# Order of the matrix products in a weights-stationary block: second part of the weights directly behind the first

## The chip, the core and the metric

The kernel runs on one core of a Trainium2 chip. The metric is the device time of one execution in microseconds, and the median of several runs is compared. A core has a matrix engine (TensorE, PE in the profile, with a row PEld for its weight loads), VectorE (DVE), ScalarE (ACT), GpSimd (POOL) and SyncE (SP), which here issues the loads from memory. Each engine works through its own instructions in order and waits on semaphores for the others.

## The reference

One layer of a diffusion backbone on 256 latent tokens and 256 context tokens of 2048 channels, all in float32. Cut to what matters here:

```python
mod = silu(c) @ w_mod + b_mod                      # shift, scale, gate
h  = modulate(rms_norm(x), shift, scale)
p_i, p_ff, p_fb, p_q, p_g, p_cv, p_cg, p_gc, p_gh = split_proj(h @ w_in)
o  = hgrn_bidir(q_prep(p_q), p_i, forget(p_ff), forget(p_fb), s_f, s_b)   # gated recurrence, 8 heads
y_h = (rms_norm(o) * silu(p_g)) @ w_o
y_c = silu(layer_norm(axial_dwconv(p_cv * sigmoid(p_cg)))) @ w_pw
x  = x + gate * rms_norm((sigmoid(p_gc) * y_c + sigmoid(p_gh) * y_h) @ w_out)
h2 = modulate(rms_norm(x), shift2, scale2)
x  = x + gate2 * rms_norm(square(relu(h2 @ w1)) @ w2)
```

The context tokens go through part of the same projection and give the recurrence's starting states s_f and s_b.

## The kernel before

**Numbers in two parts.** Every weight and every activation is split into a first part (hi, rounded to the matrix engine's fast float32 form) and the rest (lo). A product of two such numbers is taken as hi·hi + hi·lo + lo·hi, so three products stand for one.

**The weights' stream.** `Stream` brings the weights in pieces of 128 x 1024 float32 (512 KB), in the order in which they are used. `prepare` takes one piece: ScalarE copies it to `whi` (line 123), VectorE subtracts to get `wlo` (line 126). There are four buffers for each of the two (`AHEAD`, lines 117 and 118), and five for the raw pieces (line 81), which SyncE loads (line 85). `next` (line 129) keeps four pieces prepared, so the buffer of the piece in use now is filled again for the piece four later.

**Two ways to multiply.** In `tokens` (line 277) the activations are the stationary operand and the weights stream through, 512 columns at a time, by `mm3r`. In `blocks` (line 263) the weights are stationary: a piece holds eight blocks of 128 input rows and 128 output channels (cut(0) to cut(7)), and `mm2` (line 246) multiplies them with the activations of 256 tokens. For each of the eight the activation operand x(k) is 512 wide: hi of the 256 tokens, then lo. `mm2` first runs eight products with the eight blocks of whi over all 512 columns (line 252), which give hi·hi in the bank's first half and hi·lo in its second. Then it runs eight products with the blocks of wlo over the hi half alone, 256 columns, added to the bank's second half (line 254). `total` (line 225) adds the two halves when the bank is done: ScalarE copies the second half (line 228), VectorE adds (line 229).

**Where mm2 runs.** With 2048 inputs an output block takes two pieces, so two calls of `mm2`, and `blocks` calls it 160 times: 16 for the queries (line 735), 32 for the convolution's gate and value (lines 767 and 787), and for the MLP's first matrix 16 in the first quarter and 32 in each of the other three (line 995). Between the calls, `pump` lets other work in: steps of the recurrence's heads (`head`, with its small products at line 1391, each behind a copy `left` on ScalarE at line 1380 and products of x on VectorE at lines 1398, 1406 and 1407), the convolution, and sums for the gates (lines 1231 and 1244).

**What sets the order.** Each engine gets its instructions in the order of the program text as the generators emit it, with a few `issue_after` marks. A buffer is filled again only when its last reader is done: whi when the last product of line 252 in its call is done, wlo when the last of line 254 is.

Of the kernel before, what the change touches and what calls it, by code (L numbers as in the profile page):

```python
# [136 lines left out]
class Kernel:  # L137
# [108 lines left out]
    def mm2(self, bank, w, x, ks, nk):  # L246


        nc = self.nc
        cut = lambda i: slice(i * P, (i + 1) * P)  # L250
        for i, k in enumerate(ks):
            nc.tensor.matmul(bank, w[0][:, cut(i)], x(k)[2], start=(k == 0), stop=False)  # L252
        for i, k in enumerate(ks):
            nc.tensor.matmul(bank[:, T:], w[1][:, cut(i)], x(k)[0], start=False, stop=(k == nk - 1))  # L254

    def mm3r(self, out, x, w, first, last):
# [79 lines left out]
    def cut(self, pages, tb, c):  # L336

        return pages[2 * tb + c // 2][:, (c % 2) * 512:(c % 2 + 1) * 512]
# [1280 lines left out]
```

## Time and profile before

| | |
|---|---|
| median of 3 runs | 1643.31 us (1642.83 to 1644.01) |
| the profiled execution | 1643.43 us |
| its span, first to last instruction | 1641.7 us |
| granted TensorE clock | 1.000 |
| products of line 252 (512 columns) | 1280 |
| products of line 254 (256 columns) | 1280 |
| memory traffic | 227 GB/s over the span |

The profile is of one execution. Its times are microseconds from the span's start; durations of single instructions are in nanoseconds where a mean is given. A line `L252 PE MATMUL bank<-h,whi 128*128 128x512 f32 x1280 | 322.3, 394 | 0.0` says: line 252, TensorE, a product that writes bank from h and whi, 128 x 128 stationary, 128 x 512 moving, 1280 of them; together 322.3 us busy, 394 ns each; the engine idle 0.0 us just before them. Products overlap, since the next one begins before the one before has drained, so what a product costs is the distance from its start to the next one's. In a timeline several like instructions in a row are one line with their count. The chain that ended last is followed back from the last instruction, at each step to what released it.

### The profile page before, as it was taken

The numbers are of one execution on the slowest core, as the hardware profiler recorded it, in microseconds if no ns is written. First come the engines' busy times: TensorE is split into PE (matmuls) and PEld (weight loads), VectorE is DVE, ScalarE is ACT, GpSimd is POOL, SyncE is SP. The second block draws the span as 40 slices with busy tenths as digits, with TensorE's granted clock in tenths as the row PEclk, the third lists the DMA queues.
The fourth block names the chain that finished last, engine by engine and source line by source line (L and its number), as shares of the span: only waits on it lengthen the run. The fifth ranks groups of instructions, "written<-read, shape, count | busy, mean of one in ns | idle before, by whom it ended". The sixth has DMA issues, their size and how long they took to land.

```text
span 1641.7 us, 22004 instructions
## 1 busy us (share of the span) xinstructions
PE 1627.7 (99%) x8207; PEld 1357.7 (83%) x8207; DVE 1163.2 (71%) x1702; ACT 799.7 (49%) x1141; POOL 8.1 (0%) x18
## 2 busy tenths in 40 slices
PE   8999999999999999999999999999999999999998
PEld 6668888888988888888788888888888888888887
DVE  7777877777868889967887766456655665566555
ACT  6553444343554444653446665445544554346543
POOL 0000000000000000000000000000000000000000
PEclk9999999999999999999999999999999999999999
DMA  9998954444656566678887466677666666665553
GB/s 378 392 395 293 316 166 141 154 142 142 207 189 224 187 192 206 230 271 306 313 289 260 143 230 205 214 235 241 218 206 231 234 213 217 230 219 195 190 193 116
DMA packets 103484, 374.47 MB, mean 228 GB/s; under 512 B 11601, under 2 KB 11857, under 8 KB 103377
## 3 DMA queue, kind: packets, MB, share of 16 engines
q1 hardware_dynamic: 101952, 368.60, 65.8%
q0 software_dynamic: 1280, 4.21, 0.8%
q8 instruction: 64, 1.05, 0.3%
q14 instruction: 44, 0.35, 0.1%
q10 hardware_dynamic: 144, 0.26, 0.0%
HBM read 370.93 MB, written 2.10 MB: 227 GB/s over the span
## 4 chain that ended last, share of the span: by engine, by line
PE 94%; DVE 2%; DMA 2%; ACT 1%; issue 1%; SPq 0%; DVEq 0%; ACTq 0%
PE bank L185 62%; PE bank L252 18%; PE bank L254 9%; PE bank L1391 2%; DMA x<-ctx 1%; DVE wlo L126 1%; DMA rawpage<-wm 1%; PE bank L1422 0%; DMA raw<-wpw 0%; PE bank L1433 0%; PE bank L1431 0%; ACT whi L123 0%; ACT h L629 0%; SPq L498 0%; ACT xT L629 0%
## 5 line engine op out<-in xcount | busy, mean ns | idle before, releaser
L126 DVE TENSOR_TENSOR wlo<-raw,whi 128x1024 fp32r<-128x1024 f32 x488 | 594.0, 1223 | 356.2 <-ACT whi L123 348.0
L123 ACT ACTIVATE whi<-raw 128x1024 fp32r<-128x1024 f32 x488 | 513.5, 1059 | 576.9 <-PE bank L185 320.7
L185 PE MATMUL bank<-whi,h 128*128 128x512 f32 x1264 | 396.3, 391 | 0.8 <-ACT h L629 0.5
L252 PE MATMUL bank<-h,whi 128*128 128x512 f32 x1280 | 322.3, 394 | 0.0
L185 PEld LDWEIGHTS bank<-whi,h 128*128 128x128 f32 x1264 | 237.1, 188 | 51.0 <-DVE h L1080 0.7
L252 PEld LDWEIGHTS bank<-h,whi 128*128 128x128 f32 x1280 | 230.4, 189 | 41.6
L185 PE MATMUL bank<-wlo,h 128*128 128x512 f32 x632 | 246.5, 390 | 0.8 <-DVE wlo L126 0.8
L185 PE MATMUL bank<-whi,hidh 128*128 128x512 f32 x503 | 195.1, 388 | 0.0
L185 PE MATMUL bank<-wlo,hidh 128*128 128x512 f32 x503 | 195.1, 388 | 0.0
L185 PE MATMUL bank<-whi,hidl 128*128 128x512 f32 x503 | 195.0, 388 | 0.0
L254 PEld LDWEIGHTS bank<-h,wlo 128*128 128x128 f32 x1280 | 174.6, 190 | 12.6
L254 PE MATMUL bank<-h,wlo 128*128 128x256 f32 x1280 | 178.4, 282 | 0.0
L185 PE MATMUL bank<-h,whi 128*128 128x512 f32 x512 | 164.6, 402 | 0.0
L185 PEld LDWEIGHTS bank<-wlo,h 128*128 128x128 f32 x632 | 118.7, 188 | 26.6 <-DVE wlo L126 2.5
L185 PEld LDWEIGHTS bank<-whi,hidl 128*128 128x128 f32 x503 | 94.4, 188 | 19.5
L185 PEld LDWEIGHTS bank<-wlo,hidh 128*128 128x128 f32 x503 | 94.5, 188 | 19.3
L185 PEld LDWEIGHTS bank<-whi,hidh 128*128 128x128 f32 x503 | 94.5, 188 | 19.2
L185 PEld LDWEIGHTS bank<-h,whi 128*128 128x128 f32 x512 | 92.0, 189 | 21.5 <-issue 5.9
L185 PE MATMUL bank<-h,wlo 128*128 128x512 f32 x256 | 100.0, 391 | 0.0
L1244 DVE SCALAR_TENSOR_TENSOR raw<-raw,silu_row 128x1024 f32<-128x1024 f32 x64 | 76.6, 1218 | 0.2 <-DMA raw<-wmt 0.2
L1231 DVE SCALAR_TENSOR_TENSOR gacc<-raw,silu_c,gacc 128x1024 f32<-128x1024 f32 x60 | 76.6, 1277 | 0.0
L185 PEld LDWEIGHTS bank<-h,wlo 128*128 128x128 f32 x256 | 48.1, 188 | 10.6 <-DVE wlo L126 0.3
(246 smaller groups left out, 1359.8 us busy)
## 6 DMA issues: line engine op xcount, KB each, us to landing
raw<-w SPq DMA_DIRECT2D x256, 512.0 KB, 4.2
raw<-wi SPq DMA_DIRECT2D x172, 512.0 KB, 4.4
raw<-wmt SPq DMA_DIRECT2D x64, 512.0 KB, 4.2
raw<-wm SPq DMA_DIRECT2D x64, 512.0 KB, 4.5
rawpage<-wm SPq DMA_DIRECT2D x48, 512.0 KB, 8.6
raw<-wo SPq DMA_DIRECT2D x32, 512.0 KB, 4.8
raw<-wmd SPq DMA_DIRECT2D x16, 512.0 KB, 8.2
raw<-who SPq DMA_DIRECT2D x16, 512.0 KB, 4.9
```

What stands on the lines that cost most here:

```text
L123: kn.his.append(nc.scalar.activation(out=hi, in_=raw, func=AF.Copy))
L126: kn.los.append(nc.vector.tensor_tensor(lo, raw, hi.bitcast(F32), op=ALU.subtract))
L185: ins = fn(*args, **kw)
L252: nc.tensor.matmul(bank, w[0][:, cut(i)], x(k)[2], start=(k == 0), stop=False)
L254: nc.tensor.matmul(bank[:, T:], w[1][:, cut(i)], x(k)[0], start=False, stop=(k == nk - 1))
L1231: nc.vector.scalar_tensor_tensor(acc, raw, s, acc, op0=ALU.mult, op1=ALU.add)
L1244: nc.vector.scalar_tensor_tensor(raw, raw, 1.0, self.srow, op0=ALU.mult, op1=ALU.mult, accum_out=self.dot[:, 32 * j + b:32 * j + b + 1])
L1391: nc.tensor.matmul(ps[:, b * P:(b + 1) * P], w, r, start=True, stop=True)
```

## The change

In `mm2` the second loop's header is taken out, so that each product with wlo follows at once on the product with whi of the same block:

```diff
         cut = lambda i: slice(i * P, (i + 1) * P)
         for i, k in enumerate(ks):
             nc.tensor.matmul(bank, w[0][:, cut(i)], x(k)[2], start=(k == 0), stop=False)
-        for i, k in enumerate(ks):
             nc.tensor.matmul(bank[:, T:], w[1][:, cut(i)], x(k)[0], start=False, stop=(k == nk - 1))
```

The product with wlo is then at line 253. Number, size and operands of the products are the same; only their order within a call of `mm2` differs: long, short, long, short, in place of eight long and eight short.

## The prediction

> **What bounds the kernel now.** I read the page first, then its chain that ended last, then the timeline of single stretches.
>
> ```profile
> span 1641.7 us, 22004 instructions
> PE 1627.7 (99%) x8207; PEld 1357.7 (83%) x8207; DVE 1163.2 (71%) x1702; ACT 799.7 (49%) x1141; POOL 8.1 (0%) x18
> PE 94%; DVE 2%; DMA 2%; ACT 1%; issue 1%; SPq 0%; DVEq 0%; ACTq 0%
> PE bank L185 62%; PE bank L252 18%; PE bank L254 9%; PE bank L1391 2%; DMA x<-ctx 1%; DVE wlo L126 1%; DMA rawpage<-wm 1%; PE bank L1422 0%; DMA raw<-wpw 0%; PE bank L1433 0%; PE bank L1431 0%; ACT whi L123 0%; ACT h L629 0%; SPq L498 0%; ACT xT L629 0%
> L252 PE MATMUL bank<-h,whi 128*128 128x512 f32 x1280 | 322.3, 394 | 0.0
> L254 PE MATMUL bank<-h,wlo 128*128 128x256 f32 x1280 | 178.4, 282 | 0.0
> ```
>
> TensorE is the chain: 94% of it, and lines 252 and 254, the two that the change reorders, are 27% of it, some 443 us. Both rows end in 0.0: TensorE never stood idle before one of these products. So a change here counts only by how closely the 2560 products follow one another, or by a wait that it makes. The mean durations (394 and 282 ns) overlap each other, so I take differences of start times.
>
> ```profile
> 1101.70 1.98 PE L252 MATMUL bank<-h,whi 128*128 128x512 f32 x8
> 1103.51 1.11 PE L254 MATMUL bank<-h,wlo 128*128 128x256 f32 x8
> 1104.46 2.00 PE L252 MATMUL bank<-h,whi 128*128 128x512 f32 x8
> 1106.08 1.13 PEld L254 LDWEIGHTS bank<-h,wlo 128*128 128x128 f32 x8
> 1106.31 1.12 PE L254 MATMUL bank<-h,wlo 128*128 128x256 f32 x8
> 1107.14 1.70 PEld L252 LDWEIGHTS bank<-h,whi 128*128 128x128 f32 x8
> 1107.26 2.00 PE L252 MATMUL bank<-h,whi 128*128 128x512 f32 x8
> ...
> 1188.26 2.00 PE L252 MATMUL bank<-h,whi 128*128 128x512 f32 x8
> ```
>
> The columns are start, extent, engine and line. From the eight long products at 1104.46 to those at 1188.26 lie 30 calls of mm2: 83.80 / 30 = 2.793 us each, or **349.2 ns for a pair** of one long (512 columns) and one short (256). Inside a call, the long run takes 1106.31 - 1104.46 = 1.85 us and the short run 0.95 us. The first call of the stretch has 1103.51 - 1101.70 = 1.81 us for the same eight long ones.
>
> What one product costs when nothing but its own kind is around it comes from two other stretches, 21 long products in a row and 32 short ones (the tail's 256-column halves):
>
> ```profile
> 1274.30 0.39 PE L185 MATMUL bank<-whi,hidh 128*128 128x512 f32 x1
> ...
> 1279.06 1.98 PE L252 MATMUL bank<-h,whi 128*128 128x512 f32 x8
> ...
> 1629.11 0.40 PE L185 MATMUL bank<-wpage,hidh 128*128 128x256 f32 x2
> ...
> 1632.95 0.28 PE L185 MATMUL bank<-whi,hidl 128*128 128x256 f32 x1
> ```
>
> Long: 4.76 / 21 = 226.7 ns. Short: 3.84 / 32 = 120.0 ns. Their difference is 106.7 ns for 256 columns, so each product costs its columns at 0.417 ns plus 13.3 ns, whatever its length. A pair of settled products is 346.7 ns, 2.773 us for eight; mm2 takes 2.793. So **20 ns of each call belong to the switches**, and the rows say which: eight long ones after short ones take about 1.84 us instead of 1.81 (27 ns too many), and eight short ones 0.95 instead of 0.96 (about 7 too few). The long products pay after short ones everywhere; here they follow the last call of a stretch:
>
> ```profile
> 1191.06 0.40 PE L185 MATMUL bank<-whi,hidh 128*128 128x512 f32 x1
> 1191.29 0.40 PE L185 MATMUL bank<-wlo,hidh 128*128 128x512 f32 x1
> 1191.53 0.39 PE L185 MATMUL bank<-whi,hidl 128*128 128x512 f32 x1
> 1191.76 0.40 PE L185 MATMUL bank<-whi,hidh 128*128 128x512 f32 x1
> 1191.99 0.39 PE L185 MATMUL bank<-wlo,hidh 128*128 128x512 f32 x1
> 1192.22 0.39 PE L185 MATMUL bank<-whi,hidl 128*128 128x512 f32 x1
> ```
>
> Five products take 1.16 us where settled ones take 1.133, with other operands and at another line: the same 27 ns, spread over about five products, and then it is over. The first two carry most of it (0.47 us for two, 235 ns each).
>
> **The change, part by part.** It adds and removes no instruction: 160 calls issue the same 1280 + 1280 products with the same loads. It moves the short products, and with them two events: the first use of wlo comes earlier and the last use of whi later.
>
> *The cadence.* After the change every long product follows one short one, and every short one follows one long one. The trace has no such alternation, so its price needs bounds from both sides.
> - Lower end: the long one settled (226.7) and the short one as the first of a run. The short run is 7 ns too quick as a whole, and all of that would be its first product's: 113 ns. Pair 340, which is 9.2 less than now: 1280 x 9.2 = 11.8 us saved.
> - Upper end: every long one as the slowest after a run (235) and every short one at the run's 120: pair 355, 5.8 more: 7.4 us lost.
> - Value taken: each product as the first after a switch: the long one about 233 (226.7 + 6.5), the short one 113; their sum is 346.5 and thus again the sum of the settled ones, 346.7. That is the nearest row, since after the change each product is the first after a switch, and two ways of reading give it. It saves 20 ns a call. Five of the 160 calls come after long products and have 1.81 already, so 155 x 20 ns = **3.1 us saved**.
>
> *wlo earlier.* The short product's weights are now needed 0.23 us after the call begins and not 1.85 us. VectorE makes them behind ScalarE's whi:
>
> ```profile
> 1101.63 4.74 DVE L126 TENSOR_TENSOR wlo<-raw,whi 128x1024 fp32r<-128x1024 f32 x4 [5.57 <-ACT whi L123]
> 1106.51 1.06 ACT L123 ACTIVATE whi<-raw 128x1024 fp32r<-128x1024 f32 x1 [1.58 <-PE bank L252]
> 1107.60 1.23 DVE L126 TENSOR_TENSOR wlo<-raw,whi 128x1024 fp32r<-128x1024 f32 x1 [1.23 <-ACT whi L123]
> ACT whi L123 <- PE bank L252: 129.8, 86, 2.4
> ```
>
> The wlo that is ready at 1107.60 + 1.23 = 1108.83 belongs to the call four further on than that of 1104.46, at 1104.46 + 4 x 2.793 = 1115.63: a lead of 7.0 us even for the second product. The tightest place is the start of a stretch: the four made from 1101.63 serve the calls from 1104.46 on, and the first is done at about 1102.82. It leads the second product by 1.9 us. Price nothing; the cover would have to shrink by 1.9 us before it cost anything.
>
> *whi held longer.* ScalarE waits for the last long product before it overwrites a whi (86 times, the row above). That product now starts 7 x 0.347 = 2.43 us into the call instead of 1.85 - 0.23 = 1.62, so whi, the wlo behind it, and all that VectorE and ScalarE have queued behind these are 0.8 us later. The raw buffer comes free 0.8 us later too, and SP's loads that wait for it. The weights' lead of 7.0 us becomes 6.2. What has no such lead is the recurrence's heads between the calls near 460 us:
>
> ```profile
> 455.71 1.06 ACT L123 ACTIVATE whi<-raw 128x1024 fp32r<-128x1024 f32 x1
> 459.92 0.39 ACT L1380 COPY left<-x 128x256 f32<-128x256 f32 x1
> 456.80 1.23 DVE L126 TENSOR_TENSOR wlo<-raw,whi 128x1024 fp32r<-128x1024 f32 x1 [2.98 <-ACT whi L123]
> 458.27 0.55 DVE L1406 TENSOR_TENSOR x<-x,fg 128x384 f32<-128x384 f32 x1
> 458.74 0.55 DVE L1407 TENSOR_TENSOR x<-x,fg 128x384 f32<-128x384 f32 x1
> 460.36 0.71 PE L1391 MATMUL bank<-x,left 128*128 128x128 f32 x4 [0.49 <-ACT left L1380]
> PEld bank L1391 <- ACT left L1380: 2.9, 8, 0.7
> ```
>
> whi, wlo, the two products of x, left, and then TensorE, which already waits 0.49 us: a whi that is 0.8 us later makes it wait 0.8 us more. The last row counts eight such waits of the weight load in the whole kernel, most of which cost TensorE nothing. Bounds: 0 and 8 x 0.8 = 6.4 us; I take one, **0.8 us lost**, since one such wait stopped TensorE itself.
>
> Sum, against the profiled execution's own 1643.43 us (span 1641.7, 1.7 around it): 1643.4 - 3.1 + 0.8 = **1641.1 us**. The median shown is 1643.31, the same within its scatter. A measurement of this kernel can tell about 0.2% (3.3 us) from no change, so the forecast lies within that, near its lower edge: with the 0.8 in it, faster begins at a pair of 346.0 and slower at 351.2.
>
> **The rivals.**
> - *The alternation runs clean* (340 to 346 a pair). In a run of short products the next load begins as soon as a product has begun, with no pause between loads; in the alternation a load has a long product's time every second turn. For it: the load of 1107.14 starts with the last short product (1107.26 - 0.12), so the short ones are paced by loads that press on each other, and the first one, before which the load had time, is quicker. Against it: long products need about five of their kind to settle, and now never get two. Time at its end 1643.4 - 11.8 + 0.8 = 1632.4; at 343 a pair 1636.3. The Trainium skill ("TensorE: Matmul & The Clock Gate", "Architectural detail: the array is 16× 32×32, not 1× 128×128") says that TensorE's queue can pull weight loads ahead of running matmuls, which favours this rival; the trace agrees that loads are pulled ahead, but shows them ahead by one product only.
> - *The order is indifferent*: a long product owes 27 ns for eight short ones before it, 3.4 for each, and pays as much one by one. The pair stays 349.2 and the time is 1643.4 + 0.8 = 1644.2. For it: the five-product tail looks like a debt being paid. Against it: the 7 ns of the first short product come back eight times. The same page ("LDWEIGHTS (loading the stationary operand)") gives a load of 128 columns 107 ns, an estimate by which no load outlasts either product and no order matters; measured short products at 120.0 show that something more is paid.
> - *Slower: neither settles.* Every long product pays what the first two after a run pay (233 to 235) and the short one costs the 120 of the middle of a run, as if two loads always pressed on each other. Place: all 1280 pairs; price at 354 a pair 1280 x 4.8 = 6.1 us, time 1643.4 + 6.1 + 0.8 = 1650.3. It decides from a pair of 351.2 on. For it: seven of the eight short ones in a run do cost 120, and the slow start of the long ones is regular. Against it: a short one right after a long one has been the quick one.
> - *The heads' waits multiply* to the eight above: 1643.4 - 3.1 + 6.4 = 1646.7, just slower. Against it: only one of the eight stopped TensorE.
>
> **How the numbers follow.** Forecast and the indifferent order together, pairs of 346.0 to 351.2: 0.41 (0.28 and 0.13), all within 0.2%. Clean alternation below 346.0: 0.37, faster. Neither settles: 0.17, and the heads' waits: 0.05, slower. So faster 0.37, same 0.41, slower 0.22; the likeliest is the forecast, 1641.1. For the range I leave out the last tenth at each end: below, the cleanest runs under 341 a pair (1643.4 - 10.5 + 0.8 = 1633.7, rounded 1633.5); above, the unsettled ones over 352.5 (1643.4 + 4.2 + 0.8 = 1648.4, rounded 1648.5). The likeliest sign's own range, 346.0 to 349.2, is 1640.1 to 1644.2.
>
> **What would show it.** In the changed kernel's timeline, lines 252 and 253 alternate one by one; eight pairs should take 2.77 us from call to call (2.72 clean, 2.79 indifferent, 2.83 unsettled). Their rows should still end in idle 0.0. ScalarE's whi at such a call should start 0.8 us later against its beginning, and the wait for left near 460 us should grow from 0.49 to about 1.3 us. The prediction is wrong if the pair isn't near 346.7, if TensorE waits for wlo at line 253, or if the heads wait more than twice.

## The result and the profile after

| | before | after |
|---|---|---|
| median of 9 runs | 1644.01 us (1642.83 to 1645.35) | 1647.89 us (1647.25 to 1649.56) |
| ratio after / before | | 1.0025, interval 1.0016 to 1.0034 |
| the profiled execution, its span | 1643.43 us, 1641.7 us | 1647.25 us, 1645.5 us |
| granted TensorE clock | 1.000 | 1.000 |

The changed kernel is a quarter of a per cent slower: the sign that the rival *neither settles* gave, not the forecast's. The page of after, in the parts that were read of before (busy time, the chain's shares, the two groups of products):

```profile
span 1645.5 us, 22006 instructions
PE 1630.8 (99%) x8207; PEld 1356.9 (82%) x8207; DVE 1163.3 (71%) x1702; ACT 798.9 (49%) x1141; POOL 8.1 (0%) x18
PE 92%; DMA 3%; DVE 3%; ACT 1%; issue 1%; SPq 0%; DVEq 0%; ACTq 0%
L252 PE MATMUL bank<-h,whi 128*128 128x512 f32 x1280 | 454.0, 400 | 0.0
L253 PE MATMUL bank<-h,wlo 128*128 128x256 f32 x1280 | 359.6, 281 | 0.0
```

TensorE is busy 3.1 us longer (1630.8 for 1627.7) and the span is 3.8 us longer; the other engines are where they were. Both groups still end in idle 0.0, so no wait has come in front of these products. That their busy sums grew by 130 and 180 us says nothing of the cost: that is the overlap of neighbours, which alternate now. The cost is in the distance of starts, in the timeline of TensorE (start, extent, engine, line), here inside a call and then at the beginnings of two calls:

```profile
1118.90 0.40 PE L252 MATMUL bank<-h,whi 128*128 128x512 f32 x1
1119.14 0.28 PE L253 MATMUL bank<-h,wlo 128*128 128x256 f32 x1
1119.26 0.40 PE L252 MATMUL bank<-h,whi 128*128 128x512 f32 x1
1119.49 0.28 PE L253 MATMUL bank<-h,wlo 128*128 128x256 f32 x1
1119.61 0.40 PE L252 MATMUL bank<-h,whi 128*128 128x512 f32 x1
1119.84 0.28 PE L253 MATMUL bank<-h,wlo 128*128 128x256 f32 x1
1119.96 0.40 PE L252 MATMUL bank<-h,whi 128*128 128x512 f32 x1
```

```profile
1105.12 0.40 PE L252 MATMUL bank<-h,whi 128*128 128x512 f32 x1
...
1187.10 0.40 PE L252 MATMUL bank<-h,whi 128*128 128x512 f32 x1
```

Three pairs take 1119.96 - 1118.90 = 1.06 us, and 29 calls take 81.98 us: 2.827 us a call, **353.3 ns a pair** where before had 349.2 and the forecast 346.7. In nanoseconds the trace's start times repeat every three pairs:

```
long 232, short 118 | long 240, short 120 | long 236, short 114     sum 1060
```

But the same trace holds other calls, between steps of the recurrence's heads:

```profile
490.75 0.39 PE L252 MATMUL bank<-h,whi 128*128 128x512 f32 x1
...
512.94 0.39 PE L252 MATMUL bank<-h,whi 128*128 128x512 f32 x1
```

Eight calls in 22.19 us: 2.774 us each, **346.7 ns a pair**, with long products at 230 and short ones at 117. So the alternation has two patterns, and one of them is what was forecast. I call them quick and slow. Of the 160 calls, 125 run at 2.81 to 2.83 us, 13 at 2.78 or less, and 22 begin behind products of other work, after which the first long product takes 313 to 379 ns. The 13 quick ones all lie in the stretches of the convolution's gate and value.

The sums of all calls, from a call's first start to the start of what follows its last product, show where the time went:

| stretch | before, us | after, us |
|---|---|---|
| queries, 16 calls | 44.67 | 45.21 |
| gate, 16 | 46.52 | 45.82 |
| value, 16 | 45.13 | 44.90 |
| MLP, first quarter, 16 | 45.01 | 45.54 |
| MLP, each other quarter, 32 | 89.36 | 90.43 |

Together that is 3.4 us of the 3.8 between the two profiled executions. About as much as the rest is there before any reordered product runs: the first of them, in the queries, starts at 167.15 us before and at 167.66 after. The gate's stretch gains 0.7 us: there the wait of TensorE near 460 us is gone.

### The profile page after: what moved, and what is told of

It is laid out like the page before. It is cut to its first block, busy times and chain, and to the rows that moved or that the text cites. A ratio compares the mean times of both kernels' runs of the same rounds, so it can differ in the third digit from the quotient of the medians.

```text
span 1645.5 us, 22006 instructions
## 1 busy us (share of the span) xinstructions
PE 1630.8 (99%) x8207; PEld 1356.9 (82%) x8207; DVE 1163.3 (71%) x1702; ACT 798.9 (49%) x1141; POOL 8.1 (0%) x18
## 3 DMA queue, kind: packets, MB, share of 16 engines
q0 software_dynamic: 1280, 4.21, 0.7%
q8 instruction: 64, 1.05, 0.3%
## 4 chain that ended last, share of the span: by engine, by line
PE 92%; DMA 3%; DVE 3%; ACT 1%; issue 1%; SPq 0%; DVEq 0%; ACTq 0%
PE bank L185 60%; PE bank L252 18%; PE bank L253 9%; PE bank L1390 2%; DMA rawpage<-wm 1%; DVE wlo L126 1%; DMA raw<-wf 1%; DMA x<-ctx 1%; PE bank L1421 0%; DMA raw<-wpw 0%; PE bank L1432 0%; PE bank L1430 0%; DMA raw<-wmd 0%; ACT h L628 0%; SPq L497 0%
## 5 line engine op out<-in xcount | busy, mean ns | idle before, releaser
L252 PE MATMUL bank<-h,whi 128*128 128x512 f32 x1280 | 454.0, 400 | 0.0
L253 PE MATMUL bank<-h,wlo 128*128 128x256 f32 x1280 | 359.6, 281 | 0.0
L252 PEld LDWEIGHTS bank<-h,whi 128*128 128x128 f32 x1280 | 241.0, 188 | 57.6
L253 PEld LDWEIGHTS bank<-h,wlo 128*128 128x128 f32 x1280 | 242.1, 189 | 0.2
L185 PE MATMUL bank<-h,whi 128*128 128x512 f32 x512 | 164.8, 403 | 0.0
L185 PEld LDWEIGHTS bank<-h,whi 128*128 128x128 f32 x512 | 92.1, 189 | 21.5 <-issue 5.9
L185 PEld LDWEIGHTS bank<-h,wlo 128*128 128x128 f32 x256 | 48.1, 188 | 10.6 <-DVE wlo L126 0.3
```

The costliest lines, as they stand in the source:

```text
L185: ins = fn(*args, **kw)
```

## The experiments

Four explanations of the two patterns stood against each other; where an expectation uses a letter, it is one of these.
- **A**: weight loads and products fall into one of two lasting rhythms, and what goes ahead of the alternation decides which.
- **B**: a product pays for adding to the columns of the bank that the one before it has just written.
- **C**: the operands' places in memory decide, so that a given call is always quick or always slow.
- **D**: each return from short to long products costs a fixed amount.

In most of these kernels `mm2` takes its order from a table, call by call (digits are the eight blocks of whi, letters those of wlo):

```diff
-        for i, k in enumerate(ks):
-            nc.tensor.matmul(bank, w[0][:, cut(i)], x(k)[2], start=(k == 0), stop=False)
-            nc.tensor.matmul(bank[:, T:], w[1][:, cut(i)], x(k)[0], start=False, stop=(k == nk - 1))
+        ks = list(ks)
+        group = self.groups.popleft() if len(self.groups) > 1 else self.groups[0]
+        order = {1: "0a1b2c3d4e5f6g7h", 2: "01ab23cd45ef67gh", 4: "0123abcd4567efgh", 8: "01234567abcdefgh", "skew": "01a2b3c4d5e6f7gh"}[group]
+        for o in order:
+            i = "01234567abcdefgh".index(o)
+            k = ks[i % 8]
+            if i < 8:
+                nc.tensor.matmul(bank, w[0][:, cut(i)], x(k)[2], start=(k == 0), stop=False)
+            else:
+                nc.tensor.matmul(bank[:, T:], w[1][:, cut(i - 8)], x(k)[0], start=False, stop=(k == nk - 1))
```

Order 1 is that of after, 8 that of before. `groups` is set ahead of each stretch; its last entry holds for all calls that follow. With this text the long product is at line 258 and the short one at 260. "q1" to "q3" are the MLP's second to fourth quarter, "q0" its first.

### Several orders in one kernel (e1_groups)

```diff
+        self.groups = collections.deque([8])
...
+        self.groups = collections.deque([1])
...
+            self.groups = collections.deque([[1], [2], [4], ['skew']][q])
```

The first line stands ahead of the queries, the second ahead of the gate and of the value, the third ahead of the MLP's quarter q.

> Order differs by stretch: queries eight-eight, MLP quarter 0 one-one, quarter 1 two long and two short in turn, quarter 2 four and four, quarter 3 one-one shifted by one (long 0, long 1, short 0, long 2, short 1, ..., short 7). Theory A (a pair's price is a repeating pattern of TensorE that the stretch falls into at its entry): 2.793 us a call in the queries, 2.827 in quarter 0, as before and after; two-two and four-four pay the first steps after each switch (long 233, 236, 228, 232; short 113, 119, 120, 120), 2.804 both; shifted either near 2.773 or near 2.83. Rival B (the short product is slowed, or slows the next long one, because it adds to the columns that were written just before): 6.7 ns for each long product that follows a short one beside 2.773, so two-two 2.80, four-four 2.787, shifted 2.82. Rival D (a fixed price of 20 ns for each switch back to long): two-two 2.853, four-four 2.813.

1644.69 us, 1644.83 for before beside it. The queries took 2.793 us a call (order 8), q0 2.827 where nothing interrupts (order 1), q3 2.818 and 2.822 in turn (skewed). Calls of two and two in q1, then of four and four in q2, in the timeline of TensorE:

```profile
1104.64 0.40 PE L258 MATMUL bank<-h,whi 128*128 128x512 f32 x1
...
1188.24 0.62 PE L258 MATMUL bank<-h,whi 128*128 128x512 f32 x2
...
1281.79 0.63 PE L258 MATMUL bank<-h,whi 128*128 128x512 f32 x2
...
1365.99 0.63 PE L258 MATMUL bank<-h,whi 128*128 128x512 f32 x2
```

30 calls each: 83.60 / 30 = 2.787 us and 84.20 / 30 = 2.807. No set of numbers in the expectation is hit as a whole. The order is not monotonic (2.793, 2.807, 2.787 and 2.827 for groups of eight, four, two and one), so **D is out**: a fixed price for each return would rise with their number.

### Other columns of the bank (e2_half)

```diff
-            nc.tensor.matmul(bank[:, T:], w[1][:, cut(i)], x(k)[0], start=False, stop=(k == nk - 1))
+            nc.tensor.matmul(bank[:, :T], w[1][:, cut(i)], x(k)[0], start=False, stop=(k == nk - 1))
```

> The changed kernel, but the product with wlo adds to the first half of the bank in place of the second, which gives the same sum of both halves. Each half was last written at another distance in time. Theory A: nothing moves, 2.827 us a call in the MLP's quarters, total about 1647. Rival B (same columns written just before): the pair moves off 353.3, towards 346.7 (2.773 a call) if the second half's freshness is what costs.

1648.23 us. In q1, first products of two calls:

```profile
1106.09 0.40 PE L252 MATMUL bank<-h,whi 128*128 128x512 f32 x1
...
1190.89 0.40 PE L252 MATMUL bank<-h,whi 128*128 128x512 f32 x1
```

84.80 / 30 = 2.827 us, unchanged: it doesn't matter which half the short product adds to. That takes one form of B away, not all of it, since the long product before has just written both halves. The rest of B falls with e4_first below, where the same products on the same columns cost 346.7 or 353.3 ns a pair.

### Small products ahead of a stretch (e3_lead)

```diff
                     hi, lo = self.stream.next()
+                    for _ in range(self.lead if b0 == first and j == h == 0 else 0):
+                        self.nc.tensor.matmul(accs[0][:, :P], self.v["ident"], self.v["ident"], start=True, stop=True)
```

`lead` is 8 for the queries and 1, 2, 3, 4 for the MLP's quarters, 0 elsewhere.

> The changed kernel, with a few small products (128x128 float32, into a bank that is cleared right after) ahead of the first product of a stretch only: queries 8, MLP quarters 0 to 3 with 1, 2, 3 and 4. Theory A: the entry decides, so at least one of the five stretches holds 2.773 us a call (346.6 a pair) to its end, while others stay at 2.827. Rivals B and C (C: the operands' places in memory decide): all five stay at 2.827 from the second call on. The small products themselves cost about 0.1 us each.

1652.89 us. All five stretches ran at 2.827 us a call behind their first one: a miss. The trace holds 36 of the extra products at line 271, about 112 ns apart, two for each of the eighteen in the text; that is 4 of the 5 us above after. So the numbers that ran were 16, 2, 4, 6 and 8: none of these makes the alternation quick, and no odd number was tried.

### One call of another order, then the change's order (e4_first)

```diff
+        self.groups = collections.deque([8, 1])
...
+            self.groups = collections.deque([[4, 1], [2, 1], [8, 1], ['skew', 1]][q])
```

> The changed kernel, but the first call of a stretch has another order: eight-eight in the queries and in MLP quarter 2, four-four in quarter 0, two-two in quarter 1, shifted by one in quarter 3; all later calls one-one. Theory A: some of these entries give 2.773 us a call for all the later calls, others 2.827. Rivals B and C: 2.827 in every stretch from the second call on.

1645.21 us. The timeline of TensorE from the beginning of the second call on, in q1 (behind two and two) and then in q2 (behind eight and eight); the rows left out alternate in the same way:

```profile
1104.77 0.40 PE L258 MATMUL bank<-h,whi 128*128 128x512 f32 x1
1105.01 0.28 PE L260 MATMUL bank<-h,wlo 128*128 128x256 f32 x1
...
1105.82 0.39 PE L258 MATMUL bank<-h,whi 128*128 128x512 f32 x1
...
1281.49 0.40 PE L258 MATMUL bank<-h,whi 128*128 128x512 f32 x1
1281.73 0.28 PE L260 MATMUL bank<-h,wlo 128*128 128x256 f32 x1
...
1282.56 0.40 PE L258 MATMUL bank<-h,whi 128*128 128x512 f32 x1
```

Three pairs of the same order take 1.05 us behind the one call and 1.07 behind the other, and it lasts: q1 ran at 2.773 us a call in all its 31 later calls, q2 at 2.827. Behind four and four (q0) the calls were quick until other products came between them, behind the skewed order (q3) slow. q1 is the stretch that ran slow in after, with the same operands: **C is out**, and so is what was left of B. Of **A** it is shown that what goes ahead decides and that in these undisturbed stretches the pattern then stays; that loads and products make the rhythm between them is not shown by this run (two runs with half loads, below, bear on it).

### The quick entry everywhere (e5_two_first), a mixed call (e6_mixed), two and two (e7_twos)

Three whole kernels, eleven runs each. The first has one call of two and two at the head of the queries and of each quarter of the MLP (its lines are shown); the second takes the order "01ab2c3d4e5f6g7h" in every call; the third has two and two in all calls.

```diff
+        self.groups = collections.deque([2, 1])
...
+            self.groups = collections.deque([[2, 1], [2, 1], [2, 1], [2, 1]][q])
```

> The changed kernel, but in the queries and all four MLP quarters the first call of the stretch goes two long, two short in turn; all later calls one-one. Theory A: every one of these stretches then holds 2.773 us a call until other products come between two calls (quarter 0, and once in quarter 3); some 110 to 120 calls save 0.054 us against the changed kernel, so 6 us: about 1641.5 to 1642.5 where before is 1644, ratio 0.998 to 0.999. If quarter 1 of the last experiment was chance, some stretches run at 2.827 and the time is above that of before.

> Every call goes two long, two short, and then six pairs one-one, so that each call brings its own entry, also after other products. Theory A: the two-two part costs its switches (the all-two-two quarter had 2.787) and the rest 346.7 a pair: 2.773 to 2.785 a call in every stretch, gate and value stretches included, about 1641.5. Against it: a two-two part in the middle of the quick pattern may throw it out again, 2.80 to 2.83.

> Every call two long and two short in turn. From the quarter measured with this order: 2.787 a call everywhere, 6 ns less than before and 40 less than after: about 1 us below before, 1643, ratio 0.999 to 1.000.

| kernel | median of 11, us | before beside it, us | ratio, interval |
|---|---|---|---|
| e5_two_first | 1642.32 | 1644.37 | 0.9986 (0.9977 to 0.9995) |
| e6_mixed | 1644.57 | 1644.37 | 1.0001 (0.9992 to 1.001) |
| e7_twos | 1643.05 | 1644.37 | 0.9992 (0.9983 to 1.0001) |

Beginnings of the second and the thirty-second call of q1 in e5_two_first, in its timeline:

```profile
1103.76 0.40 PE L258 MATMUL bank<-h,whi 128*128 128x512 f32 x1
...
1186.96 0.40 PE L258 MATMUL bank<-h,whi 128*128 128x512 f32 x1
```

83.20 / 30 = **2.773 us a call**, the forecast's number. The queries, q1 and q2 ran so throughout; q0 only until other work came between the calls at 978 us, and q3 up to its fourteenth call (about 1492 us). In all, 111 calls were quick, 27 slow, and 22 began behind other products. With five changed calls the order of after is 2.1 us below before; after was 3.9 above it, so in all the five calls are worth about 6 us, from two comparisons. By call sums, half of the gain over before is not the entries': 0.9 of 1.8 us lies in the gate's and the value's stretches, which run as in after.

In the mixed kernel the calls took turns:

```profile
1106.02 0.63 PE L258 MATMUL bank<-h,whi 128*128 128x512 f32 x2
1106.49 0.39 PE L260 MATMUL bank<-h,wlo 128*128 128x256 f32 x2
...
1108.80 0.62 PE L258 MATMUL bank<-h,whi 128*128 128x512 f32 x2
1109.26 0.40 PE L260 MATMUL bank<-h,wlo 128*128 128x256 f32 x2
...
1111.62 0.63 PE L258 MATMUL bank<-h,whi 128*128 128x512 f32 x2
```

2.78 us, then 2.82, and so on, where 2.773 to 2.785 was expected: two and two is no key by itself. Where its two short products took 116 and 113 ns the pairs behind them were quick; where they took 113 and 119 they were slow. A call that is entered from slow pairs comes out the first way and one entered from quick pairs the second, so they take turns. The two and two of e7_twos stays at 2.787 us a call, as expected; its interval includes no change against before.

### Entering again behind the interruption (e9_reenter)

e5_two_first, with two and two again in the ninth call of q0 and the fifteenth of q3, behind the interruptions.

```diff
+            self.groups = collections.deque([[2, 1, 1, 1, 1, 1, 1, 1, 2, 1], [2, 1], [2, 1], [2, 1, 1, 1, 1, 1, 1, 1, 1, 1, 1, 1, 1, 1, 2, 1]][q])
```

> As the kernel with two long, two short in the first call of the queries' and MLP's stretches, and the same order again for the call after an interruption: the ninth call of quarter 0 and the fifteenth of quarter 3. Theory A: 2.773 us in the 17 calls of quarter 3 behind it, where it was 2.827, and possibly in the last seven of quarter 0: 0.9 to 1.3 us less, about 1641.2, ratio 0.998. If the place in the stretch mattered and not the entry, quarter 3 stays at 2.827 there.

1642.24 us, before 1644.09, ratio 0.9988 (0.9979 to 0.9997): no gain over e5_two_first. Both calls ended on short products of 113 and 119 ns, and the calls behind them ran slow, as the mixed kernel's reading says; this run's expectation missed. The groups inside these calls show why: the two short products of the four groups take 116 and 112, 113 or 114 and 119, 116 and 112 or 113, 113 and 119 ns. Each group of two and two turns one state into the other, and four of them, entered from slow pairs, come back to slow. Entered from settled long products, four end on 116 and 112 (e5_two_first). One group behind slow pairs leads to quick ones in every second call of the mixed kernel; no run used that behind an interruption and then kept to one-one.

### Half a weight load for the short products (e8_cols), for the long ones (e10_long_cols)

In e8_cols 15 of 16 short products load 64 columns of weights in place of 128 (queries, q1, q2); the output channels left out lack that part of the lo·hi term. In e10_long_cols 14 of 16 long products do, in the same stretches, which leaves out half of what they add. Queries run in order 8, q1 in order 1, q2 in order 1 behind a first call of two and two; q0 and q3 keep whole loads, q3 in order 1 behind a first call of four and four. Where a load is halved, the product that uses it is half as wide too, so these runs can't tell the one from the other.

```diff
+                n = self.cols if k < nk - 1 else P
+                nc.tensor.matmul(bank[:n, T:], w[1][:, cut(i - 8)][:, :n], x(k)[0], start=False, stop=(k == nk - 1))
...
+                n = self.cols if 0 < k < nk - 1 else P
+                nc.tensor.matmul(bank[:n], w[0][:, cut(i)][:, :n], x(k)[2], start=(k == 0), stop=False)
```

> Measures what the weight load adds. In the queries (order eight-eight), MLP quarter 1 (one-one) and quarter 2 (two-two first, then one-one) 15 of 16 short products use only 64 of their 128 weight columns, which leaves half of that correction out; quarter 0 one-one and quarter 3 four-four first, then one-one, whole. If the 13.3 ns that each product takes beside its columns is the weight load running next to it, half a load takes 6.7: in the queries the settled short product falls from 120.0 to 113.3 and the long ones stay at 226.7; in the quick pattern a pair falls from 346.7 to about 340. If the 13.3 ns belong to the product itself, nothing moves. Theory A says nothing on the size in the slow pattern, but a load that is shorter changes the phase, so quarter 1 may leave 353.3. Quarter 3 should hold 2.773 by its four-four entry.

> The counterpart: 14 of 16 long products use only 64 of their 128 weight columns (half of what these would add is left out), the short ones all 128. Queries eight-eight, MLP quarter 1 one-one, quarter 2 two-two first and then one-one; quarters 0 and 3 whole (one-one, and four-four first). If a short product is paced by the load that runs next to it, it costs 113.3 beside a half load: with the long one's 226.7 the pair is 340, 2.72 us a call, in quarters 1 and 2, apart from the full-width ones. If not the load but the short product itself is slow, the pair stays near 347. In the queries the long ones stay at 226.7, the short run at 120.

One run each: 1640.92 and 1640.9 us. Queries of e8_cols, the eights of a whole call:

```profile
203.30 2.00 PE L258 MATMUL bank<-h,whi 128*128 128x512 f32 x8
205.14 1.08 PE L261 MATMUL bank<-h,wlo 128*64 128x256 f32 x8
206.06 2.00 PE L258 MATMUL bank<-h,whi 128*128 128x512 f32 x8
```

The short run takes 0.92 us (before: 0.95), settled products 113 to 114 ns for 120; the long run still takes 1.84, its slow beginning unchanged. In q1 every call took 2.772 to 2.778 us, behind long products too, and so did those of q2 from its third on (the second 2.790): the slow pattern is gone. But 2.777 us is 347 ns a pair; the 340 that were expected for the quick pattern did not come.

q2 of e10_long_cols, pairs with half and then with whole weights for the long product, and two of the weight loads (PEld):

```profile
1183.18 0.39 PE L259 MATMUL bank<-h,whi 128*64 128x512 f32 x1
1183.40 0.28 PE L261 MATMUL bank<-h,wlo 128*128 128x256 f32 x1
...
1184.20 0.39 PE L259 MATMUL bank<-h,whi 128*64 128x512 f32 x1
...
1184.76 0.28 PE L261 MATMUL bank<-h,wlo 128*128 128x256 f32 x1
1184.77 0.19 PEld L259 LDWEIGHTS bank<-h,whi 128*128 128x128 f32 x1
1184.88 0.40 PE L259 MATMUL bank<-h,whi 128*128 128x512 f32 x1
1185.11 0.28 PE L261 MATMUL bank<-h,wlo 128*128 128x256 f32 x1
1185.23 0.40 PE L259 MATMUL bank<-h,whi 128*128 128x512 f32 x1
1185.47 0.28 PE L261 MATMUL bank<-h,wlo 128*128 128x256 f32 x1
1185.47 0.14 PEld L259 LDWEIGHTS bank<-h,whi 128*64 128x64 f32 x1
1185.59 0.40 PE L259 MATMUL bank<-h,whi 128*64 128x512 f32 x1
1185.82 0.28 PE L261 MATMUL bank<-h,wlo 128*128 128x256 f32 x1
1185.94 0.39 PE L259 MATMUL bank<-h,whi 128*64 128x512 f32 x1
```

Three pairs with half the load take 1184.20 - 1183.18 = 1.02 us: 340 ns a pair, 227 + 113. Two whole loads for long products in a row (those of 1184.88 and 1185.23) make the next three pairs (233 + 117) + (241 + 119) + (233 + 117), 1.06 us. So the half loads take away both the short product's 117 to 120 ns and the long one's 233 to 241.

What a whole load costs does not fall on the product beside it. Each load starts beside the product before its own. The short product at 1184.76 has the first whole load beside it (1184.77) and takes 1184.88 - 1184.76 = 0.12 us, 113 ns in the trace's nanoseconds; the one at 1185.47 has a half load beside it and takes 119. In the same way the first short product of before's runs has a whole load beside it and takes 113. The cost comes a product or two late and is spread over long and short ones.

In the queries, where half loads run beside the long products of a run, eight of them take 1.84 us (the starts' differences are 224 to 236 ns), in the first call too, where whole loads took 1.81. The expectation of settled 226.7 missed there, and no run shows why.

q3 of both kernels, with whole loads, ran quick in all its 31 later calls, as expected, also behind the interruption at its fourteenth call. First products of the fifteenth and the last call of e8_cols:

```profile
1493.36 0.40 PE L258 MATMUL bank<-h,whi 128*128 128x512 f32 x1
...
1540.51 0.40 PE L258 MATMUL bank<-h,whi 128*128 128x512 f32 x1
```

47.15 / 17 = 2.774 us a call, where e5_two_first and e9_reenter ran at 2.827. Behind four and four the long products take 230 ns and the short ones 117, behind two and two 231, 112, 233 and 117 in turn: two forms of the quick pattern with the same sum, and here the first form was followed by quick calls behind the interruption and the second by slow ones.

## Why the prediction was wrong, and where it was right

**The cadence: the value taken failed.** The bounds, 340 to 355, hold both patterns that came, and the quick one has the value taken, 346.7, though not its parts: the long products take 230 ns and the short ones 117, not 233 and 113. What failed is the step "each product as the first after a switch", with about 233 and 113 as its fixed price. That takes a product's cost to depend on its kind and its neighbour. The runs show that it depends on the state in which the alternation is entered: the same products in the same order cost 346.7 or 353.3 a pair, for a whole stretch (e4_first). From long products, with which the clean stretches start, or from a call of eight and eight it goes to 353.3. Before's undisturbed calls can't show this, since their switches are eight products apart and the long ones settle in between.

**The split of the two costs failed too.** The forecast read 226.7 and 120.0 as 0.417 ns a column and 13.3 ns whatever the length. In rows of half loads a short product takes 113 (e8_cols' queries, e10_long_cols' pairs), half of a settled long one's 226.7: 0.443 ns a column and no fixed part that these rows show. Long products don't get cheaper with half loads beside them (226 to 230 in most of e8_cols' pairs). So the settled short product's other 6.7 ns go with whole loads that follow one another closely. They are not a price that each short product pays for the load beside it, since the first of a run has a whole load beside it and takes 113; from before's rows one couldn't tell how much of them an alternation would bring back.

**The rival that came true** is *neither settles*, given 0.17. It asked for 354 a pair and put the point of decision at 351.2; measured 353.3 in the slow pattern, and from call sums 125 x 33 ns = 4.2 us more in the slow calls (2.827 less 2.793 us each). Its reason was only half right: the short products (118, 120, 114) come near what the middle of a run costs, but the long ones go up to 240, which no long product of a run in before's undisturbed calls does.

**The clean alternation** (340 to 346) did not come with these loads; its lower end, 340, is what e10_long_cols shows with half the long products' loads. The Trainium skill ("TensorE: Matmul & The Clock Gate", "Architectural detail: the array is 16× 32×32, not 1× 128×128") says that weight loads can be pulled ahead of running matmuls. The runs agree: each load starts beside the product before its own (the load for the product of 1184.88 at 1184.77 in e10_long_cols). They also show that this is not free: 120.0 ns a product in a run of short ones with whole loads, 113 to 114 with half ones.

**The order is indifferent** (349.2) fell: e1_groups alone has four different costs for four orders. The 107 ns of its estimate are not what the trace shows of a load: those of lines 252 and 254 last 189 and 190 ns on average, so a load does outlast the 113 to 120 ns from a short product to the next.

**wlo earlier: right.** Line 253 ends in idle 0.0, as the price of nothing had it.

**whi held longer: right in its size, wrong in the chain behind it.** ScalarE near 460 us, first before and then after (the bracket is the idle time before and what ended it), with TensorE's products of after:

```profile
458.95 1.06 ACT L123 ACTIVATE whi<-raw 128x1024 fp32r<-128x1024 f32 x1 [2.19 <-PE bank L252]
459.92 0.39 ACT L1380 COPY left<-x 128x256 f32<-128x256 f32 x1
```

```profile
457.60 1.06 ACT L123 ACTIVATE whi<-raw 128x1024 fp32r<-128x1024 f32 x1 [0.75 <-PE bank L252]
459.55 0.41 ACT L1379 COPY left<-x 128x256 f32<-128x256 f32 x1 [0.89 <-DVE x L1406]
460.82 1.06 ACT L123 ACTIVATE whi<-raw 128x1024 fp32r<-128x1024 f32 x1 [0.86 <-PE bank L252]
460.74 0.61 PE L1390 MATMUL bank<-x,left 128*128 128x128 f32 x4
```

whi starts 2.95 us behind its call's beginning (457.60 after 454.65), where before had 458.95 - 456.82 = 2.13: 0.8 later, as predicted. But the chain whi, wlo, x, left of the forecast is not what held left in before. There the second x had ended at 458.74 + 0.55 = 459.29, and left started only at 459.92, directly behind a whi on ScalarE itself that had waited 2.19 us for the long products of line 252. In after, left stands ahead of the next whi: it starts at 459.55, as soon as x is done, and the products of line 1390 start at 460.74 behind no wait, in place of 0.49 us of it. So instead of 0.8 us lost, the gate's stretch gained 0.7. Each engine works through its instructions in order, so this is another order of them: the traces of before and after differ in it here on ScalarE and on VectorE, although their program text is the same. That the text alone sets the order is therefore too simple, and what moved it is not shown.

**The sum.** Forecast -3.1 and +0.8; measured, from the table of call sums, +4.3 in the queries and the MLP (0.54 + 0.53 + 3 x 1.07) less 0.7 and 0.2 in the gate's and the value's stretches, where the 13 quick calls are. That the time lies inside the range is partly luck: the range's upper end stood for 352.5 ns a pair, less than the slow pattern's 353.3. With 353.3 in all 1280 pairs and the forecast's 0.8 us it would have been 1643.4 + 5.2 + 0.8 = 1649.4, outside. The 13 quick calls and the wait that went away kept it inside.

**What stays open.** What the two patterns are inside the array is not shown. Behind products of other work a few nanoseconds go with them, though not strictly: in after all seven calls whose first long product takes 316 ns run slow, of the 13 with 313 to 315 ten run quick and three slow (476.85, 979.95 and 989.73 us), and the two with 332 and 379 run quick. That would fit a phase between loads and products; no run sets that phase by itself. A kernel with quick calls behind all interruptions was not built: what the record has for it is the four and four of e8_cols' and e10_long_cols' q3, which passes the interruption there, though not those of q0 in e4_first, and the single group of two and two behind slow pairs in the mixed kernel.

## What to carry to other kernels

Where two kinds of products alternate, don't price one by the first product after a switch in another order: the alternation can have a steady rhythm of its own, so put a short stretch of it on the chip and read some thirty calls, not three. If a trace shows the same sequence at two speeds, change what goes ahead of it before changing the sequence: five calls of another order were worth about 6 us here. And before a delay is carried along a chain of several engines, look for what the waiting instruction really stood behind: here it was its own engine's order, and that order was another one in the changed kernel.

## What the runs showed of the hardware

- A settled product of 512 columns takes 226.7 ns (21 in a row in before) and one of 256 columns 120.0 (32 in a row). With 64 columns of weights for each in place of 128, the one of 256 columns takes 113 to 114 (e8_cols).
- A load of 128 columns of weights lasts 188 to 190 ns on average and one of 64 columns 134 (before, e10_long_cols); all but some twenty of the 2560 start within 0.01 us of the start of the product before their own, and what it costs can come a product or two later.
- The first long products behind eight short ones take about 234, 236, 228, 232, 231 ns before they settle at 227, and half loads for the short products don't change that (e8_cols).
- The same alternation of 512 and 256 columns holds one of two rhythms, 346.7 or 353.3 ns a pair, for a whole undisturbed stretch of 31 calls. Behind a call of two and two its last two short products tell which: 115 or 116 ns and then 112 or 113 came ahead of the quick one, 113 and 119 or 120 ahead of the slow one; each group of two and two turns the one into the other (e6_mixed, e9_reenter).
